# The end of a feed-forward block: turning the next norm's first rows by DMA, and keeping one product's weights for another

## The chip, the cores and the metric

The kernel runs on one core of a Trainium2 chip. The metric is the device time of one execution in microseconds, the median of several runs. TensorE (PE) multiplies, VectorE (DVE) and ScalarE (ACT) work elementwise, GpSimd (POOL) and SyncE (SP) mostly issue transfers here, and the transfers run on 16 DMA engines. Each engine executes its own list of instructions in order.

## The reference

Two layers, each of three residual updates of `x` (512 positions by 1024 channels, float32), and a final norm:

```python
for l in range(DEPTH):                                   # DEPTH = 2
    x = x + 0.5 * swiglu(rms_norm(x, ffn1_norm[l]), ffn1_w_in[l], ffn1_w_out[l])
    x = x + mixer(rms_norm(x, mix_norm[l]), ...)         # attention over a grid, a 2-D DFT, gates
    x = x + 0.5 * swiglu(rms_norm(x, ffn2_norm[l]), ffn2_w_in[l], ffn2_w_out[l])
return rms_norm(x, final_norm)

def swiglu(x, w_in, w_out):                              # w_in 1024 x 5632, w_out 2816 x 1024
    g, u = jnp.split(x @ w_in, 2, axis=-1)
    return (jax.nn.silu(g) * u) @ w_out
```

There are thus four feed-forward blocks (FFNs). The change touches the second product, `(silu(g) * u) @ w_out`, of each.

## The kernel before, in words

**Precision.** Every large product is made of three TensorE passes over float32 values that are split into a high and a low part: high by high, high by low, low by high. A weight granule of 128 x 1024 (or 128 x 512) is loaded into a tile `raw`; ScalarE writes its high part `whi` (line 191, or 186 with the sign turned) and VectorE the low part `wlo` (line 194 or 187). There are three buffers each for `whi` and `wlo`, so granules are prepared two ahead of the one that TensorE works on. Lines 502, 503 and 505 are the three passes.

**Seven products.** The products are done by a Strassen scheme: the two operands are cut into 2 x 2 blocks, and seven products (numbered 1 to 7) of sums and differences of blocks take the place of eight. In the output product of an FFN the 2816 hidden features are cut into two halves of three chunks (3, 4 and 4 tiles of 128). The order is product 1 for its three chunks, then product 2 for its three, then for each chunk the products 5, 6, 7 and 3, and last product 4 for its three: 21 steps, `i` = 0 to 20 in the code. This text calls these 21 steps the end of an FFN. `hl` and `comb` (lines 322, 323 and 744) prepare the activations of a step (`c1h`, `c1l` and so on), `update` (line 750) adds a finished product to `x` from PSUM, on VectorE.

**Weights.** The blocks of `w_out` are called a, b, c and d. Product 1 uses -a, product 2 uses b, product 5 uses d - c, of which c comes by a second transfer that adds to the tile already loaded (GpSimd's queue, line 150; the sign is in the data), product 6 adds a to that, product 7 uses c and a in the same way, product 3 adds b on VectorE (line 164), product 4 uses d alone. Each product loads what it needs anew, so b is loaded for product 2 and once more for product 3. Plain loads are issued by SyncE (line 148) into the tile `raw`, of which there are nine in an FFN. A list of items in the order of use (`stage_items`) says what is loaded when; `Stream.fetch` loads up to eight items ahead of the one being prepared.

**Hidden features to columns.** The last hidden blocks of the up phase have to be turned before the end can use them. `apart` copies a block's 16-bit words apart on ScalarE (line 347, tile `zs`), a transposing DMA issued by SyncE (line 348) turns them into `zt`, and `joined_words` puts the words together again (line 357, two copies). In the end this happens for two blocks, z2 and then z1, joined behind the steps 3 (z1) and 5 (z2).

**The next norm's rows.** The next stage needs `x` turned as well, in four quarters, `quad(i, j)`. Each quarter takes eight TensorE transposes of 128 x 128 into PSUM (line 414), four ScalarE copies with the norm's gain (line 417), and a split into high and low part (418 and 419). In the ends of the first three FFNs `quad(0, 0)` stands behind step 6, `quad(1, 1)` and `quad(0, 1)` behind the first step of product 4. The last FFN has none of these: it goes over to the final norm instead. The turned halves are kept in tiles of the tags `xh` and `xl`, two buffers each (8 KB a partition). The current norm's own halves sit in them until the up phase has ended.

**Order.** Except in blocks that are marked as scheduled by hand, the order of instructions on each engine is made by a planner when the kernel is built: it issues an instruction when its operands and a free buffer are there, in the order of the program among those that are ready. `tc.keep_in_program_order` pins an instruction behind those traced before it on its engine.

## Time and profile before

| | |
|---|---|
| three runs | 1849.15, 1852.43, 1852.99 us; median 1852.43 |
| the profiled execution | 1849.34 us, of which 1847.6 us lie between its first and last instruction (the span) |
| mean granted TensorE clock | 0.998 |
| the ends of the four FFNs, from their first matmul to the end of the last | 107.47, 107.48, 108.71 and 105.15 us |
| they begin in the span at | 219.57, 816.28, 1135.32 and 1734.10 us |
| read from HBM | 367.88 MB |

All numbers of the trace are of one profiled execution, and positions are microseconds from the start of its span. A row of the timeline begins with the start and the duration of one instruction (or of several alike, with their count), then engine, line, operation, and the tiles written and read; in square brackets stands how long the engine was idle before, and what ended that. `PEld` is the loading of the stationary operand, `SPq` and `POOLq` are transfers issued by SyncE and GpSimd. Matmuls are pipelined, so one lasts 0.39 us while the next starts after some 0.23. In the rows by group, the number behind the bar is busy time in us, then the mean of one in ns.

### The profile page before, as it was taken

Reading aid. Unit: us, or ns where it says so; the run is one execution under the profiler, and the core shown is the slowest. Engines: PE = TensorE matmul, PEld = TensorE weight load, DVE = VectorE, ACT = ScalarE, POOL = GpSimd, SP = SyncE. Lnnn points to the kernel's source line nnn. Section 1 sums busy time; section 2 is a strip of 40 time slices with the busy share of each in tenths; the row PEclk is TensorE's granted clock in tenths of the full one; section 3 lists DMA queues with packets and bytes.
Section 4 is the critical chain, followed back from the end, with each engine's and each line's share of the span. In section 5 each row is a group of like instructions: output and inputs, shape, how many; then the busy total and the mean of one; then the engine's idle time right before and its main releaser. Section 6 shows DMA issues by size and latency. Waiting matters only on the chain.

```text
span 1847.6 us, 24580 instructions
## 1 busy us (share of the span) xinstructions
PE 1836.8 (99%) x8850; PEld 1528.9 (83%) x8850; DVE 1603.4 (87%) x1950; ACT 1312.9 (71%) x1785; POOL 173.3 (9%) x212
## 2 busy tenths in 40 slices
PE   9999999999999999999999999999999999999998
PEld 7888888888888888888888888888888888888886
DVE  7878899786989987889998888997869899888899
ACT  6777875668576777777667778766776776777865
POOL 0010010100111010001010100101001101010010
PEclk9999999999999999999999999999999999999999
DMA  9898799934897798979888886989258866989795
GB/s 306 223 236 218 192 276 272 229 107 125 232 235 174 183 220 222 213 203 280 248 194 221 223 223 195 270 285 213 69 183 212 227 176 170 236 219 223 199 285 150
DMA packets 198282, 395.72 MB, mean 214 GB/s; under 512 B 103760, under 2 KB 103888, under 8 KB 198160
## 3 DMA queue, kind: packets, MB, share of 16 engines
q1 hardware_dynamic: 168912, 294.23, 50.2%
q0 software_dynamic: 28816, 99.38, 30.0%
q8 instruction: 69, 1.13, 0.2%
q10 hardware_dynamic: 432, 0.55, 0.1%
q14 instruction: 53, 0.43, 0.1%
HBM read 367.88 MB, written 2.11 MB: 200 GB/s over the span
## 4 chain that ended last, share of the span: by engine, by line
PE 96%; DVE 2%; ACT 1%; issue 0%; DMA 0%; SPq 0%; DVEq 0%; ACTq 0%
PE A L502 10%; PE A L505 10%; PE A L503 10%; PE o L505 7%; PE o L503 7%; PE o L502 7%; PE B L502 5%; PE B L503 5%; PE B L505 5%; PE ps L316 4%; PE ps L317 3%; PE ps L318 3%; PE C L503 3%; PE C L502 3%; PE C L505 3%; PE tr L414 1%
## 5 line engine op out<-in xcount | busy, mean ns | idle before, releaser
L194 DVE TENSOR_TENSOR wlo<-raw,whi 128x1024 fp32r<-128x1024 f32 (+1 forms) x534 | 630.3, 1190 | 176.4 <-ACT whi L191 175.8
L191 ACT ACTIVATE whi<-raw 128x1024 fp32r<-128x1024 f32 (+1 forms) x534 | 546.0, 1033 | 256.5 <-PE A L503 53.8
L150 POOL DMA_DIRECT2D raw<-in_wst_dram x166 | 144.4, 894 | 1350.9 <-DMA raw<-in_wst_dram 810.8
L164 DVE TENSOR_TENSOR raw<-raw,raw 128x1024 f32<-128x1024 f32 (+1 forms) x148 | 176.1, 1190 | 2.0
L503 PE MATMUL A<-whi,xl 128*128 128x512 f32 x400 | 155.7, 389 | 0.0
L502 PE MATMUL A<-whi,xh 128*128 128x512 f32 x400 | 155.7, 389 | 0.0
L357 ACT ACTIVATE at<-zt 128x1024 uint16<-128x1024 uint16 (+2 forms) x96 | 110.4, 1167 | 15.6 <-DMA zt<-zs 15.4
L186 ACT ACTIVATE whi<-raw 128x1024 fp32r<-128x1024 f32 (+1 forms) x83 | 85.8, 1037 | 46.9 <-issue 12.8
L505 PE MATMUL A<-wlo,xh 128*128 128x512 f32 x400 | 115.1, 389 | 0.0
L187 DVE SCALAR_TENSOR_TENSOR wlo<-raw,whi 128x1024 fp32r<-128x1024 f32 (+1 forms) x83 | 98.2, 1191 | 12.1 <-ACT whi L186 12.1
L505 PEld LDWEIGHTS A<-wlo,xh 128*128 128x128 f32 x400 | 75.1, 188 | 15.6
L503 PEld LDWEIGHTS A<-whi,xl 128*128 128x128 f32 x400 | 75.1, 188 | 15.5
L502 PEld LDWEIGHTS A<-whi,xh 128*128 128x128 f32 x400 | 75.1, 188 | 15.4
L503 PE MATMUL C<-whi,xl 128*128 128x512 f32 x208 | 81.0, 389 | 0.0
L503 PE MATMUL B<-whi,xl 128*128 128x512 f32 x208 | 81.0, 389 | 0.0
L502 PE MATMUL C<-whi,xh 128*128 128x512 f32 x208 | 80.9, 389 | 0.0
L502 PE MATMUL B<-whi,xh 128*128 128x512 f32 x208 | 80.9, 389 | 0.0
L347 ACT ACTIVATE zs<-th 128x1024 uint16<-128x1024 uint16 x80 | 79.5, 1041 | 0.8 <-DVE th L731 0.8
L724 ACT ACTIVATE th<-sn,rh 128x512 f32<-128x512 f32 x80 | 55.0, 715 | 34.2 <-DVE sn L577 33.4
L572 ACT ACTIVATE sn<-A 128x512 f32<-128x512 f32 x104 | 59.1, 585 | 25.1 <-PE A L505 25.0
L505 PE MATMUL C<-wlo,xh 128*128 128x512 f32 x208 | 59.8, 389 | 0.0
L505 PE MATMUL B<-wlo,xh 128*128 128x512 f32 x208 | 59.8, 389 | 0.0
(428 smaller groups left out, 4680.5 us busy)
## 6 DMA issues: line engine op xcount, KB each, us to landing
raw<-in_wst_dram SPq DMA_DIRECT2D x468, 512.0 KB, 5.9
raw<-in_wst_dram POOLq DMA_DIRECT2D x176, 512.0 KB, 7.9
bm<-in_bias_dram SPq DMA_DIRECT2D x16, 512.0 KB, 4.3
raw<-in_wst_dram SPq DMA_DIRECT2D x30, 256.0 KB, 4.1
x<-in_xin_dram SPq DMA_DIRECT2D x4, 512.0 KB, 10.2
raw<-in_wst_dram POOLq DMA_DIRECT2D x8, 256.0 KB, 8.8
dft<-in_dft_dram POOLq DMA_DIRECT2D x8, 256.0 KB, 11.1
gb<-in_gbias_dram SPq DMA_DIRECT2D x4, 512.0 KB, 9.1
```

The lines of the kernel that those rows point to most:

```text
L150: G.dma_start(out=self.t, in_=wst[GRAN_AT[self.plus]][:, 0 : self.n], accum_op=ALU.add)
L164: V.tensor_tensor(self.raw.t, self.raw.t, self.add.t, ALU.add)
L186: S.activation(hi, t, AF.Copy, scale=-1.0)
L187: self.last = V.scalar_tensor_tensor(lo, t, -1.0, hi.bitcast(F32), ALU.mult, ALU.subtract)
L191: S.activation(hi[:, cs], t[:, cs], AF.Copy)
L194: self.last = V.tensor_tensor(lo[:, cs], t[:, cs], hi[:, cs].bitcast(F32), ALU.subtract)
L316: PE.matmul(ps, lh, rh, start=start, stop=False, skip_group_check=again)
L347: S.activation(s[:, h], words[:, h], AF.Copy)
L357: S.activation(to[:, w], t[:, w], AF.Copy)
L502: PE.matmul(ps, lh, rh, start=start, stop=False, skip_group_check=again)
L503: PE.matmul(ps, ll, rh, start=False, stop=False, skip_group_check=again)
L505: PE.matmul(ps, lh, rl, start=False, stop=stop, skip_group_check=again)
```

## The change

**Product 2's weights.** The six granules of block b (three chunks, two granules each) are made once per FFN, as `kept`, and both product 2 and product 3 use them. They have a home instead of a `raw` tile: two tiles of the tag `xh` and one of `xl`, that is, buffers in which the current norm's halves lay. They are loaded by GpSimd's queue. `fetch` stops in front of such an item until `homes[0]` is set, which is done at the beginning of the end; behind step 6 it is taken back.

**The next norm's first rows.** `quad(0, 0)` no longer uses TensorE. `turned_quad` does it in five pieces behind the steps 6, 8, 10, 11 and 12: words apart on ScalarE, the transposing DMA on SyncE (in program order), words joined on ScalarE, four scalings by the gain on ScalarE (from SBUF, in place), the split on ScalarE and VectorE. The words before and after the turn lie in the second `xl` buffer. The other two quarters of an end stay as they are, and so does the last FFN in this respect.

```diff
-                self.t = raw_pool[0](self.n)
+                self.t = homes[0](*self.home, self.n) if self.home else raw_pool[0](self.n)
+                queue = G if self.home else nc.sync
...
-                    nc.sync.dma_start(out=self.t[:, cs], in_=wst[GRAN_AT[self.key]][:, cs])
+                    queue.dma_start(out=self.t[:, cs], in_=wst[GRAN_AT[self.key]][:, cs])
...
+            if kept:
+                r["b"] = kept
...
+            kept = [
+                [Raw((s, "ob", c, g), n, home=(c, g)) for g, n in enumerate(out_sizes(c))] for c in range(3)
+            ]
             for order in ((1,), (2,), (5, 6, 7, 3), (4,)):
                 for c in range(3):
                     summed = s == (L - 1, 2) and c == 2
-                    strassen(s, lambda q: "o" + q, c, out_sizes(c), order, summed)
+                    strassen(s, lambda q: "o" + q, c, out_sizes(c), order, summed, kept=kept[c])
...
             while self.loaded < min(to, n) and self.items[self.loaded].stage <= self.stage:
+                if self.items[self.loaded].raw.home and not homes[0]:
+                    break
...
+        def turned_quad(self, i, j, st):
+
+            js = slice(j * 256, (j + 1) * 256)
+            s = st[:, 0].rearrange("p (h q b f) -> p h q b f", h=2, q=4, b=2)
+            t = st[:, 1].rearrange("p (h q c) -> p h q c", h=2, q=4)
+            words_apart(x[:, 2 * j : 2 * j + 2, i * T : (i + 1) * T], s)
+            yield
+            tc.keep_in_program_order(turned_words(s, t)[1])
+            yield
+            raw = self.raw[i, j] = slot(F32, "xr")
+            joined_words(raw, t)
+            yield
+            self.tiles(i)
+            for k in range(4):
+                S.activation(raw[:, k, :], raw[:, k, :], AF.Copy, scale=self.gain(4 * i + k))
+            yield
+            split(self.h[i][:, :, js], self.l[i][:, :, js], raw)
+            yield
...
+        kept = [np_.tile([P, 4, T], F32, tag="xh", name=nm("ob"), bufs=2) for _ in range(2)]
+        words = np_.tile([P, 2, 2048], U16, tag="xl", name=nm("zq"), bufs=2)
+        kept.append(np_.tile([P, 4, T], F32, tag="xl", name=nm("ob"), bufs=2))
+        homes[0] = lambda c, g, n: kept[c][:, 2 * g : 2 * g + n // T, :].rearrange("p k t -> p (k t)")
+        quad00 = nxt.turned_quad(0, 0, words)
...
-            if i == 6 and not late:
-                nxt.quad(0, 0)
+            if i == 6:
+                homes[0] = None
+            if i in (6, 8, 10, 11, 12) and not late:
+                next(quad00)
```

In the last FFN's third chunk product 3 takes b by an adding transfer in both versions; there the change only moves product 2's load. `apart` is split into `words_apart` and `turned_words`, with the same work.

More of the change, by code (lines that the diff above doesn't have):

```diff
@@ L203, in add, with strassen @@
             items.append(Item(*a, stage=st, **k))
-        def strassen(s, name, idx, sizes, order, dma=False, behind=None):
+        def strassen(s, name, idx, sizes, order, dma=False, behind=None, kept=None):
             def key(q, g):
@@ L313, in encoder_kernel @@
     raw_pool = [None]
+    homes = [None]
     def mm3(ps, lh, ll, rh, rl, start, stop, again=False):
```

16 lines of the change are left out of this document (10 added, 6 removed).

## Prediction

> **What bounds the kernel now.** I read the page's first part, then the four stretches in which the change acts, then the timelines inside them. "End 1" to "end 4" are the four output products of the FFNs, from their first matmul to their last; a "step" is one of an end's 21 (product, chunk) pairs, a "granule" one load of 128x1024 or 128x512 weights.
>
> ```profile
> span 1847.6 us, 24580 instructions
> PE 1836.8 (99%) x8850; PEld 1528.9 (83%) x8850; DVE 1603.4 (87%) x1950; ACT 1312.9 (71%) x1785; POOL 173.3 (9%) x212
> core 0: us, PE busy (x) PEld busy (x) DVE busy (x) ACT busy (x) POOL busy (x), PEclk, DMA share, GB/s
> 219.57:327.04 107.47, 107.47 (x488) 89.25 (x486) 104.21 (x108) 77.26 (x97) 12.63 (x15) 1.00 0.95 269
> 816.28:923.76 107.48, 107.48 (x488) 89.25 (x486) 106.90 (x111) 78.00 (x98) 12.96 (x15) 1.00 0.92 256
> 1135.32:1244.03 108.71, 108.33 (x487) 88.94 (x486) 104.29 (x108) 76.84 (x97) 12.56 (x15) 1.00 0.93 264
> 1734.10:1839.25 105.15, 105.15 (x463) 86.38 (x461) 101.70 (x116) 71.27 (x87) 12.12 (x14) 1.00 0.81 219
> ```
>
> Over the whole span TensorE is the bound. In the ends it has company: in end 2 VectorE works 106.90 of 107.48 us, and the DMA engines are over nine tenths busy in three of the four. So a microsecond taken from TensorE there counts only where VectorE is early enough. How early it is stands in the timelines of VectorE and TensorE at the last granule of product 3, where `wlo` is written by line 194 and read by line 505 (ends 1, 2 and 3):
>
> ```profile
> 306.60 1.22 DVE L194 TENSOR_TENSOR wlo<-raw,whi 128x1024 fp32r<-128x1024 f32 x1
> 308.45 0.62 PE L505 MATMUL o<-wlo,c3h 128*128 128x512 f32 x2
> 903.23 1.21 DVE L194 TENSOR_TENSOR wlo<-raw,whi 128x1024 fp32r<-128x1024 f32 x1
> 905.17 0.62 PE L505 MATMUL o<-wlo,c3h 128*128 128x512 f32 x2
> 1223.30 0.98 PE L505 MATMUL o<-wlo,c3h 128*128 128x512 f32 x3 [0.38 <-DVE wlo L194]
> ```
>
> In end 1 the low part is ready at 306.60 + 1.22 = 307.82 and used at 308.45: 0.63 us to spare. In end 2 it is 905.17 - 904.44 = 0.73. In end 3 it comes too late, and TensorE sits idle. That is the first thing to keep in mind: the margins are under a microsecond.
>
> **The change part by part.** *Transposes leave TensorE.* Three ends (not the fourth, which has no next norm to prepare) lose the eight transposes of the next norm's block (0, 0):
>
> ```profile
> 253.57 1.03 PE L414 MATMUL tr<-ident,x 128*128 128x128 f32 x8
> 254.36 0.49 PE L502 MATMUL o<-whi,c6h 128*128 128x512 f32 x1
> 254.68 0.40 PE L503 MATMUL o<-whi,c6l 128*128 128x512 f32 x1
> ```
>
> From 253.57 to the next matmul it is 0.79 us, and that one is followed after 0.32 instead of about 0.23 as elsewhere: 0.88 us an end, 2.6 us in all. The transposes stand ahead of product 3, and VectorE's work up to there is the same in number: the split of the block (one 1.2 us operation) only moves from behind step 6 to behind step 12. So TensorE would reach product 3's last granule 0.88 us earlier and wait there for what VectorE lacks. Realised: 0.63 in end 1, 0.73 in end 2, nothing in end 3. Term one: **-1.4 us**.
>
> *ScalarE takes over the turning.* Each of the three ends gets two copies of 16-bit words, one DMA transpose, two copies that join them; the four scalings stay, now from SBUF.
>
> ```profile
> L347 ACT ACTIVATE zs<-th x80: 1036/1042/1060, 69.8 to 1742.1; 128x1024 uint16<-128x1024 uint16 x80
> L357 ACT ACTIVATE at<-zt x96: 477/1358/1380, 82.9 to 1758.0; 128x1024 uint16<-128x1024 uint16 x64, 128x256 uint16<-128x256 uint16 x16, 128x768 uint16<-128x768 uint16 x16
> L348 SPq DMA_TRANSPOSE zt<-zs x44: 1346/3350/7060, 71.9 to 1743.2; - x44
>   DMA zt<-zs: 15.4, 8
> ```
>
> That is 2 x 1.04 + 2 x 1.36 = 4.8 us of ScalarE an end. The cover is its idle time, 107.47 - 77.26 = 30 us in end 1, so I put it at nothing. If a copy stands just ahead of a `whi` that VectorE waits for, VectorE loses up to the 1.36 us of that copy; the last row (idle time before line 357 by releaser) says that where the wait is for the transposing DMA it was 15.4 / 8 = 1.9 us each, in 8 cases. On SyncE the new transpose stands in program order behind the loads issued by step 8, and holds the queue 3.35 us in the middle; the loads behind it are later by that, but see the next part.
>
> *Six loads fewer an end, six on another queue.* Product 3 no longer loads its second addend; product 2 loads it once, to tiles that the up phase has left, on GpSimd's queue.
>
> ```profile
> raw<-in_wst_dram SPq DMA_DIRECT2D x468, 512.0 KB, 5.9
> raw<-in_wst_dram POOLq DMA_DIRECT2D x176, 512.0 KB, 7.9
> zt<-zs SPq DMA_TRANSPOSE x44, 5.4
> dft<-in_dft_dram POOLq DMA_DIRECT2D x8, 256.0 KB, 11.1
> 1792.06 2.01 ACT L191 ACTIVATE whi<-raw 128x1024 fp32r<-128x1024 f32 x2 [3.19 <-DMA raw<-in_wst_dram]
> 1793.16 1.23 DVE L194 TENSOR_TENSOR wlo<-raw,whi 128x1024 fp32r<-128x1024 f32 x1 [2.52 <-ACT whi L191]
> 1194.60 1.23 DVE L194 TENSOR_TENSOR wlo<-raw,whi 128x1024 fp32r<-128x1024 f32 x1 [0.60 <-ACT whi L191]
> ```
>
> Five loads of 512 KB and one of 256 KB go away, 2.9 MB of the some 29 MB (107.47 us x 269 GB/s) of an end; in the last end only two chunks of three gain. More than that, these granules leave the nine `raw` buffers, for which SyncE's loads queue, so the loads of products 5, 6 and 7 start earlier. Late landings show in the last three rows: VectorE idle 2.52 us in end 4 and 0.60 in end 3. End 3 gets back its 0.60. End 4 has 462 matmuls; the chain of waits shows 24 of them in
>
> ```profile
> 268.72 0.91 PE o L505 x4
> 274.16 0.91 PE o L505 x4
> ```
>
> 5.44 us, so 462 take 104.8, and 105.15 - 104.8 = 0.35 is all that end 4 can return. Term two: **-0.95 us**.
>
> *The dead tiles' price.* The loads of product 2 were in flight before the end began; now the first may start only when the up phase has read its last, about the end's first matmul. ScalarE wants the first granule 11.2 us into end 1 (230.78):
>
> ```profile
> 230.78 1.56 ACT L191 ACTIVATE whi<-raw 128x1024 fp32r<-128x1024 f32 x2
> 234.27 1.07 ACT L191 ACTIVATE whi<-raw 128x1024 fp32r<-128x1024 f32 x1 [0.98 <-PE o L503]
> 235.24 2.58 ACT L357 ACTIVATE at<-zt 128x1024 uint16<-128x1024 uint16 x2
> GB/s 131 323 225 16 66 104 296 313 89 27 120 290 283 120 315 357 270 281 296 80 60 230 285 197 219 203 241 263 274 356 411 422 413 375 219 192 224 219 142 219
> ```
>
> With 7.9 us to landing it is there after some 9 us, so the weights themselves cost nothing. Below, an earlier start could gain at most the 0.8 us that VectorE idles early in end 1; above, by the 11.1 us of the nearest plain load on that queue, it would be about 12 us, near 1 us late. But the last row (40 slices of 0.75 us of 219.57 to 249.50) shows where they run: beside the two transposes of the last hidden block, issued 3.1 and 9.1 us into the end. The second is what line 357 needs at 235.24, and ScalarE is in order: behind it stands `whi` of product 2's second chunk. End 3 already shows what a transfer on GpSimd's queue does beside that transpose:
>
> ```profile
> 1144.39 3.20 SPq L348 DMA_TRANSPOSE zt<-zs  x1
> 1146.83 1.73 POOL L150 DMA_DIRECT2D raw<-in_wst_dram  x2 [49.58 <-DVE at L744]
> 1151.98 2.59 ACT L357 ACTIVATE at<-zt 128x1024 uint16<-128x1024 uint16 x2 [0.89 <-DMA zt<-zs]
> 1155.51 1.23 DVE L194 TENSOR_TENSOR wlo<-raw,whi 128x1024 fp32r<-128x1024 f32 x1 [1.81 <-ACT whi L191]
> 829.72 2.59 ACT L357 ACTIVATE at<-zt 128x1024 uint16<-128x1024 uint16 x2 [1.23 <-DMA zt<-zs]
> 238.75 1.23 DVE L194 TENSOR_TENSOR wlo<-raw,whi 128x1024 fp32r<-128x1024 f32 x1 [0.80 <-ACT whi L191]
> ```
>
> The block arrived about 1151.98, 7.6 us after its issue, and VectorE stood still 1.81 us instead of end 1's 0.80; those 1.0 us are most of the 1.24 by which end 3 is longer than end 1. I bound this cost by nothing (the slices at 3 and 6 to 8 us into the end, with 16 and 27 GB/s, have room for all of it) and by 3 us an end (below). Nearest is end 3's row: 1.0 us each for ends 1 and 4. End 2 waited 1.23 for the block and lost no VectorE time early (busy in all of 816.28 to 846.20), so 0; end 3 has paid. Term three: **+2.0 us**.
>
> The Trainium skill, "DMA: Bandwidth & Descriptors", section "Issuing engines are not separate DMA queues", says that DMAs started by any engine run on the same 16 DMA engines and interleave; "Queues, rings and completion order" adds that each engine goes round-robin between the queue rows by packets. End 3's rows agree (the turned block landed later beside GpSimd's transfer). By that rule alone the second transpose would halve its rate as long as product 2's weights flow, which speaks against this change and is the first rival below.
>
> **Sum.** -1.4 - 0.95 + 2.0 = -0.3 us on the profiled execution's own 1849.34 (span 1847.6): 1849.0. That execution stands 3.1 us under the median of the three runs, 1852.43, so on the median it is 1852.1.
>
> **The rivals.** *Slower: the last hidden block is late in every end.* GpSimd's ring then has up to six loads in flight from about 1 to 12 us. At end 1's 269 GB/s, 2.9 MB take 10.8 us; if a third falls ahead of the second transpose, it lands 3.6 us later. ScalarE waits, VectorE idles as long, and it has no time to give back (104 to 107 of 107 us). Minus what the row of end 1 leaves, about 3 us an end: 4 x 3 = 12, with the first two terms +9.7: about 1862. It decides where the block lands later than 15.7 us into the end. For it: the 0.89 and 1.23 us waits exist today. Against: the empty slices, and two dead tiles (product 3 of the up phase was their last reader) free 5 us before the end.
>
> *Faster: everything asked for is realised.* More prefetch keeps VectorE from ever idling; then 2.6 + 1.24 + 0.35 = 4.2 us go, 1848.2. For it: the margins are missed by tenths only. Against: end 2's VectorE has 0.58 us idle in all, so its share could come only from work that moves behind the end.
>
> *Slower: the turned rows are late for ScalarE.* The new joining copies come two steps (8.2 us) behind their DMA, which lands after 5.4 us in the middle if SyncE's queue is free. If not, 1.9 us each by the idle row, up to twice in three ends: +5 to +11 with VectorE full, 1857 to 1863 before the other terms.
>
> *Slower: GpSimd's weights late for product 2.* TensorE waits if the first granule lands later than about 13.5 us into the end; at 2 us an end, +8: 1860.
>
> Per "DMA: Bandwidth & Descriptors" of the Trainium skill, "Anatomy of one DMA", a 512 KB load would take about 2.0 + 524288 / 436e3 = 3.2 us (an estimate); by it the last rival falls away, but the rows here say 5.9 and 7.9.
>
> **How the numbers follow.** Forecast 0.37, its own range 1849 to 1856. Late hidden block 0.24, late turned rows 0.07, late weights 0.05: slower together 0.36. Faster 0.27, though its price lies only just outside 0.2% (3.7 us), which is about what this kernel's measurement tells from no change; the three runs themselves lie 3.8 us apart, so an end without late landings could give more on the median than in this profile. The range reaches from just under the faster case to most of the late hidden block: 1847.5 to 1861.
>
> **What would show it.** 72 - 24 = 48 transposes in the ends at line 414's place, ScalarE some 14 us busier, DMA some 10 MB less. Right: TensorE idle before `wlo` in product 3 of ends 1 and 2 of some 0.2 us, and ends of about 107. Wrong to the slow side: line 357 idle for the DMA in the first 20 us of every end, or `xr` copies waiting for it. Wrong to the fast side: ends 1 to 3 near 106.5 us, VectorE never idle in them.

## The result and the profile after

The changed kernel takes 1913.63 us in the median (1892.33 to 1921.82, six runs) against 1851.95 us of the kernel before on the same chip: slower by about 62 us, where 1852.1 was forecast. The ratio, which leaves out the slowest of the six runs because it was in a slower state, is 1.0308, with a 95% interval from 1.0282 to 1.0335. The profiled execution took 1911.5 us, its span is 1909.7 us, 62.1 more than before.

The page's first part, then the stretches of the four ends (from first matmul to last) in the same columns as before:

```profile
span 1909.7 us, 24487 instructions
PE 1845.7 (97%) x8826; PEld 1533.8 (80%) x8826; DVE 1603.6 (84%) x1950; ACT 1325.1 (69%) x1797; POOL 186.2 (10%) x236
220.12:334.51 114.39, 109.61 (x480) 90.37 (x479) 103.91 (x108) 79.81 (x97) 11.95 (x15) 0.97 0.88 255
824.61:952.42 127.81, 108.99 (x479) 89.87 (x478) 106.02 (x110) 81.77 (x102) 12.25 (x15) 0.92 0.86 198
1163.98:1287.77 123.79, 108.83 (x479) 89.83 (x478) 103.82 (x108) 79.25 (x97) 11.99 (x15) 0.93 0.86 210
1781.76:1901.33 119.57, 106.59 (x463) 87.29 (x461) 101.74 (x117) 71.77 (x87) 11.40 (x14) 0.94 0.77 179
```

VectorE has the same work as before (1603.6 against 1603.4 us), and three of the four ends move fewer bytes (end 1 moves 29.1 MB, before 28.9). Still the ends are 6.9, 20.3, 15.1 and 14.4 us longer, together 56.8 of the 62.1. A further 3.9 us lie between end 3 and end 4 (from 1287.77 to 1781.76 it is 493.99 us, before it was 490.07). In the ends TensorE is no longer busy all the time, and its granted clock fell. The waits of TensorE and ScalarE say where (engine, what was waited for; us in total, times, the longest):

```profile
PE o L538 <- ACT whi L192: 51.5, 4, 18.8
ACT at L374 <- DMA zt<-zs: 76.7, 10, 21.2
```

There is one wait of TensorE in each end, four in all, and 51.5 us together. ScalarE's wait for the transposing DMA (line 374 is the old line 357) rose from 15.4 us in 8 cases to 76.7 in 10. The timeline of end 2, which begins at 824.61, shows how the one becomes the other. ScalarE, then TensorE, then what SyncE and GpSimd issue:

```profile
836.15 0.63 ACT L192 ACTIVATE whi<-ob 128x512 fp32r<-128x512 f32 x1 [0.26 <-PE o L539]
858.02 2.53 ACT L374 ACTIVATE at<-zt 128x1024 uint16<-128x1024 uint16 x2 [21.24 <-DMA zt<-zs]
861.54 1.04 ACT L192 ACTIVATE whi<-ob 128x1024 fp32r<-128x1024 f32 x1
862.64 0.79 PE L538 MATMUL o<-whi,c2h 128*128 128x512 f32 x1 [18.82 <-ACT whi L192]
827.68 11.24 SPq L362 DMA_TRANSPOSE zt<-zs  x1
839.63 16.28 SPq L362 DMA_TRANSPOSE zt<-zs  x1
819.19 2.15 POOL L149 DMA_DIRECT2D ob<-in_wst_dram  x4 [0.65 <-PE B L539]
821.31 0.93 POOL L151 DMA_DIRECT2D raw<-in_wst_dram  x1
825.08 1.08 POOL L149 DMA_DIRECT2D ob<-in_wst_dram  x2 [2.83 <-PE A L541]
833.16 0.88 POOL L151 DMA_DIRECT2D raw<-in_wst_dram  x1 [7.01 <-DVE wlo L188]
835.02 0.87 POOL L151 DMA_DIRECT2D raw<-in_wst_dram  x1 [0.97 <-DVE wlo L188]
```

The first transpose holds SyncE for 11.24 us, so the second is issued at 839.63, 15 us into the end instead of 9, and it holds SyncE for another 16.28 us. ScalarE, in order, waits 21.24 us for the turned block, and behind that stands the `whi` that TensorE needs. On GpSimd's queue there are not only product 2's six plain loads (`ob`, line 149): the adding loads of the products 5 and 7 (line 151) come at -3.3, +8.5 and +10.4 us of this end, and one more before that, at -6.9. In the kernel before, the first adding load of this end came at +10.9. Between its issue and its landing the trace has for the two transposes 26.6 and 18.4 us (5.2 and 4.3 before). What the DMA engines did from 837 to 850 us (bytes a second in 40 slices, then packets, MB and share of the 16 engines by queue; q1 is SyncE's, q0 GpSimd's):

```profile
GB/s 71 54 24 26 25 24 23 28 23 71 19 31 37 50 293 58 49 37 44 35 35 22 58 54 69 28 162 121 58 55 81 68 55 102 50 83 109 101 147 93
q1 hardware_dynamic: 1210, 0.33, 85.3%
q0 software_dynamic: 167, 0.51, 43.5%
```

The engines are counted as busy throughout, and move 0.84 MB in 13 us. So this is no shortage of bandwidth: transposes and the other transfers hold each other up. In the ends 3 and 4 it is alike (26.1 and 25.3 us for the first transpose). End 1 is another case: the first transpose took 17.0 us there while the engines moved 4.74 MB, at 278 GB/s, so the many bytes beside it are enough to explain its delay.

After each wait TensorE is slow for some microseconds. These are the stretches of the wait, of the 5 us behind it, and of what follows (the last three columns are granted clock, DMA share and GB/s):

```profile
843.00:862.50 19.50, 0.81 (x4) 0.35 (x2) 0.83 (x1) 4.45 (x5) 1.70 (x2) 0.59 1.11 160
862.50:867.50 5.00, 4.86 (x12) 3.85 (x13) 4.73 (x6) 5.00 (x6) 0.00 (x0) 0.53 0.89 170
867.50:890.00 22.50, 22.50 (x101) 18.60 (x100) 22.50 (x26) 16.06 (x23) 0.85 (x1) 1.00 0.48 119
```

With the clock at 0.53, twelve matmuls start in 5.0 us, 427 ns apart instead of 227. Over the four ends 40 matmuls start late in this way, 8.5 us together. 51.5 of waiting and 8.5 of slow clock are 60.0; the ends grew by 56.8, so some 3 us were gained in them elsewhere. The experiments find these 3 us again.

### The profile page after: what moved, and what is told of

It is laid out like the page before. It is cut to its first block, busy times and chain, and to the rows that moved or that the text cites. A ratio compares the mean times of both kernels' runs of the same rounds, so it can differ in the third digit from the quotient of the medians.

```text
span 1909.7 us, 24487 instructions
## 1 busy us (share of the span) xinstructions
PE 1845.7 (97%) x8826; PEld 1533.8 (80%) x8826; DVE 1603.6 (84%) x1950; ACT 1325.1 (69%) x1797; POOL 186.2 (10%) x236
## 4 chain that ended last, share of the span: by engine, by line
PE 93%; DMA 3%; ACT 2%; DVE 1%; issue 0%; SPq 0%; DVEq 0%
PE A L538 10%; PE A L541 10%; PE A L539 10%; PE o L538 7%; PE o L539 7%; PE o L541 7%; PE B L539 5%; PE B L538 5%; PE B L541 5%; PE ps L325 3%; PE ps L326 3%; PE ps L327 3%; DMA zt<-zs 3%; PE C L538 2%; PE C L539 2%; PE C L541 2%
## 5 line engine op out<-in xcount | busy, mean ns | idle before, releaser
L195 DVE TENSOR_TENSOR wlo<-raw,whi 128x1024 fp32r<-128x1024 f32 (+1 forms) x510 | 603.2, 1192 | 169.8 <-ACT whi L192 169.3
L192 ACT ACTIVATE whi<-raw 128x1024 fp32r<-128x1024 f32 (+1 forms) x510 | 522.4, 1035 | 245.9 <-PE A L539 56.3
L374 ACT ACTIVATE at<-zt 128x1024 uint16<-128x1024 uint16 (+2 forms) x96 | 110.1, 1164 | 76.8 <-DMA zt<-zs 76.7
L165 DVE TENSOR_TENSOR raw<-raw,raw 128x1024 f32<-128x1024 f32 x126 | 151.4, 1202 | 2.0
L187 ACT ACTIVATE whi<-raw 128x1024 fp32r<-128x1024 f32 (+1 forms) x83 | 85.7, 1035 | 45.7 <-issue 12.5
L538 PE MATMUL o<-whi,c2h 128*128 128x512 f32 x88 | 38.6, 439 | 51.5 <-ACT whi L192 51.5
L538 PEld LDWEIGHTS A<-whi,xh 128*128 128x128 f32 x400 | 75.1, 188 | 15.4
L538 PEld LDWEIGHTS o<-whi,c2h 128*128 128x128 f32 x88 | 18.8, 213 | 57.3 <-ACT whi L192 53.2
## 6 DMA issues: line engine op xcount, KB each, us to landing
ob<-in_wst_dram POOLq DMA_DIRECT2D x20, 512.0 KB, 11.6
```

The source lines that it names most:

```text
L165: V.tensor_tensor(self.raw.t, self.raw.t, self.add.t, ALU.add)
L187: S.activation(hi, t, AF.Copy, scale=-1.0)
L192: S.activation(hi[:, cs], t[:, cs], AF.Copy)
L195: self.last = V.tensor_tensor(lo[:, cs], t[:, cs], hi[:, cs].bitcast(F32), ALU.subtract)
L374: S.activation(to[:, w], t[:, w], AF.Copy)
L538: PE.matmul(ps, lh, rh, start=start, stop=False, skip_group_check=again)
```

## The experiments

In each of them the kernel before ran on the same chip. "T1" and "T2" are the two transposes of the last hidden block; positions with a sign count from the start of an end. Issue and landing are those of the single transfer in the trace.

### Which half of the change

`turn` leaves the weights as they were, `keep` leaves the next norm's rows as they were:

```diff
# turn: product 2 and 3 load b into raw tiles, no homes
-                    strassen(s, lambda q: "o" + q, c, out_sizes(c), order, summed, kept=kept[c])
+                    strassen(s, lambda q: "o" + q, c, out_sizes(c), order, summed)
# keep: the first quarter is turned on TensorE
-            if i in (6, 8, 10, 11, 12) and not late:
-                next(quad00)
+            if i == 6 and not late:
+                nxt.quad(0, 0)
```

> Only the next norm's first rows are turned by a DMA; product 2's and product 3's weights are loaded by SyncE into raw tiles as before the change. Theory 1 (the last hidden block's transposing DMA is starved by transfers on GpSimd's queue, which only the kept weights bring forward): no end has TensorE idle for more than 1 us before product 2's second chunk, the time is 1847 to 1853 us. Theory 2 (the new transpose and its copies on ScalarE are what makes the ends late): the ends keep at least half of what they lost, above 1880 us.

> Only product 2's weights are kept for product 3, in the dead tiles and on GpSimd's queue; the next norm's first rows are turned on TensorE as before the change. Theory 1 (last hidden block's transposing DMA starved): TensorE idle 4 to 19 us in each end before product 2's second chunk, 1905 to 1925 us, as with the whole change. Theory 2 (the new transpose): about 1852 us.

Measured: `keep` 1907.85 us, 1.0315 [1.0255, 1.0374]; `turn` 1870.99 us, 1.0118 [1.0087, 1.0148]. With `keep`, TensorE waits in the same four places:

```profile
PE o L538 <- ACT whi L192: 38.9, 4, 13.5
```

So the kept weights carry the loss, and theory 2 falls. But `turn` isn't free either, though theory 1 had it so (1847 to 1853 us). There T1 and T2 land as before (T2 at +13.4 to +15.1), and it is the new transpose `zq` that ScalarE waits for; that is taken up again below.

### Which transfers: the queue, or the earlier adding loads

```diff
# sync: the kept weights on SyncE's queue
-                queue = G if self.home else nc.sync
+                queue = nc.sync
# held: a kept granule also occupies a raw tile until its high part is made
+                if self.home:
+                    self.d = raw_pool[0](self.n)
+                    nc.sync.dma_start(out=self.d[:, 0:16], in_=wst[GRAN_AT[self.key]][:, 0:16])
...
+            if self.raw.home and self.raw.d is not None:
+                S.activation(self.raw.d[:, 0:16], self.raw.d[:, 0:16], AF.Copy)
```

> The whole change, but product 2's kept weights are loaded by SyncE's queue into the same dead tiles. Theory 1a (the six plain loads on GpSimd's queue starve the transposes): the last hidden block lands within 18 us of the end's start, TensorE waits under 2 us an end, 1850 to 1860 us. Theory 1b (it is the adding loads of product 5 on GpSimd's queue, which start up to 15 us earlier because six granules no longer take raw tiles): they still start early, the block still lands more than 20 us into the end, above 1885 us.

> The whole change, with GpSimd's queue for product 2's weights, but each of the six granules also holds a raw tile (64 bytes a row of it are loaded by SyncE, and ScalarE copies them in place after the granule's high part), so the loads that follow get their raw tiles no earlier than before the change. Theory 1a (plain loads on GpSimd's queue starve the transposes): stalls of 4 to 19 us an end stay, above 1890 us. Theory 1b (adding loads too early): the adding loads start 11 us or more into an end, the block lands within 18 us, 1850 to 1862 us.

Measured: `sync` 1857.47 us, 1.0029 [1.0013, 1.0045]; `held` 1889.04 us, 1.0227 [1.017, 1.0283]. TensorE's wait at the disputed place, for `sync` and then for `held`:

```profile
PE o L538 <- ACT whi L192: 2.7, 1, 2.7
```

```profile
PE o L544 <- ACT whi L195: 19.4, 4, 8.1
```

`sync` is in the range that 1a gave, and T2 lands at +16.5 to +17.3. But it does not separate the two theories: two adding loads of GpSimd still start ahead of each end there (-7.0 to -4.2), and the next only at +15.1 to +15.9, where the change has them at +6.8 to +8.5. `held` lies between the two theories: its adding loads start at +4.3 to +6.5 instead of -6.9, but still 6 to 8.5 us earlier than before the change, and T1 lands at +16.9 to +19.1. `held` also has a disturbance of its own, 1.3 to 3.2 us an end in product 1, whose loads queue behind the raw tiles. Neither theory alone gives both numbers. What the kernels have in common is when GpSimd's queue runs empty in the first part of an end (the second row is a run of the next part):

| kernel, end | last transfer of GpSimd's batch lands | T1 lands |
|---|---|---|
| `held_best` (below), ends 1 to 4 | +8.0 to +10.1 | +11.8 to +12.1 |
| `dose_g`, end 4 | +12.3 | +14.0 |
| `keep`, end 1 | +18.0 | +19.4 |
| the change, end 1 | +18.7 | +20.1 |
| the change, end 2 | +30.6 | +29.7 |

### The disputed cost by itself

The kernel before gets extra loads of 512 KB at the start of the ends, into the dead tiles, used by nobody: none in end 1, then 2, 4 and 6. `dose_g` issues them from GpSimd, `dose_a` from ScalarE, `dose_s` from SyncE, whose queue also carries the transposes; `dose_p` pairs a plain load by SyncE with an adding one by GpSimd. `dose_g12` and `dose_s12` have 4, 8 and 12 of them. `dose_split` is `dose_s` with T1 and T2 issued by ScalarE.

```diff
         ps = {}
+        spare = [np_.tile([P, 4, T], F32, tag=t, name=nm("sp"), bufs=2) for t in ("xh", "xh", "xl")[3 - extra[0] :]]
+        for t in spare:                      # the 12s: spare + spare
+            for g in range(2):
+                G.dma_start(                 # dose_a: S; dose_s: nc.sync; dose_p: nc.sync, then G with accum_op=ALU.add
+                    out=t[:, 2 * g : 2 * g + 2, :].rearrange("p k t -> p (k t)"),
+                    in_=wst[GRAN_AT[((0, 1), "ob", 2, g)]][:, 0:1024],
+                )
+        extra[0] += 1
# dose_split, also
-            turned.append((apart(z), j, f0))
+            turned.append((apart(z, S if f0 == 2 + 4 * (NB - 1) else None), j, f0))
```

> The kernel before, with 0, 2, 4 and 6 plain loads of 512 KB in the ends 1 to 4, issued by GpSimd at the end's start into the dead tiles and used by nobody. It prices GpSimd's queue beside the two transposes of the last hidden block with nothing else moved. If transfers on GpSimd's queue starve a transpose: the block lands 2 to 4 us after the last of them, later from end to end, and ends 3 and 4 lose 2 to 10 us each. If only bytes count (2.1 MB more in end 3, 3.1 MB in end 4, against some 29 MB): the block lands at most 3 us later and no end loses over 3 us.

> The same 0, 2, 4 and 6 extra loads, issued by ScalarE. If any second queue beside SyncE's starves the transposes, the block lands as late as with GpSimd's loads; if it is GpSimd's queue alone, the block lands within 18 us of the end's start in all ends. ScalarE stands at the loads until the dead tiles are free, so some of the time may be its own wait.

> The same 0, 2, 4 and 6 extra loads, issued by SyncE ahead of the transposes on their own queue. If it is a second queue beside the transposes that starves them, the block lands within 18 us of the end's start in all ends, later only by the time that the loads take (under 3 us), and the ends lose under 2 us each.

> The kernel before, with 0, 2, 4 and 6 pairs of extra loads in the ends 1 to 4: a plain load of 512 KB by SyncE into a dead tile, and an adding load of 512 KB by GpSimd on top of it; nobody uses them. If adding loads are what starves a transpose, end 3 and end 4 lose clearly more than with as many plain loads on GpSimd's queue (which lost nothing in end 3 and some 3.5 us in end 4): the block lands more than 20 us into end 4, and end 4 loses 5 to 20 us. If adding and plain loads on GpSimd's queue are alike, end 3 loses under 2 us and end 4 under 5.

> The kernel before, with 0, 4, 8 and 12 plain loads of 512 KB by GpSimd at the start of the ends 1 to 4, each destination written twice in the ends 2 to 4; nobody uses them. If any transfer on GpSimd's queue holds a transpose back, the first transpose of end 4 lands 1 to 2 us after the last of the twelve, about 20 us into the end, and end 4 loses 5 us or more. If only adding loads do, it lands within 12 us although the plain loads are still under way. If the mutual slowing needs adding loads, the twelve take no more than some 12 us each and end 4 loses under 10 us, against 29.8 us with six adding loads.

> The kernel before, with 0, 4, 8 and 12 plain loads of 512 KB by SyncE, the queue of the transposes, at the start of the ends 1 to 4 (the second half of them overwrite the first). If the queue matters and not the bytes, a transpose takes 4 to 8 us from its issue in every end, and what is lost is that it is issued later, behind the loads. If bytes matter, the first transpose of end 4 takes 15 us or more, as with twelve by GpSimd (20.3 us).

> The kernel before, with the two transposes of the last hidden block issued by ScalarE instead of SyncE, and 0, 2, 4 and 6 plain loads of 512 KB by SyncE at the start of the ends 1 to 4. If any queue beside the transposes' own holds them back, the first transpose of end 4 takes 9 us or more and lands shortly after SyncE's loads have landed, and already in end 1 it takes longer than the 7.7 us of before, since SyncE's usual loads are now on another queue. If it is GpSimd's queue alone, it takes 4 to 8 us in every end. ScalarE stands while it issues a transpose, so some time is lost that way.

Measured, a single time each, with the kernel before at 1849.91 to 1850.54 us beside them. The ends of the profile before were 107.48, 108.71 and 105.15 us (2 to 4), and T1 took 5.1 us in end 4:

| kernel | time, us | ends 2, 3, 4, us | T1 in end 4: issue to landing, us |
|---|---|---|---|
| `dose_g` | 1853.3 | 107.65, 107.97, 108.56 | 11.0 |
| `dose_a` | 1856.8 | 107.47, 109.73, 112.18 | 11.7 |
| `dose_s` | 1854.16 | 110.73, 107.58, 107.21 | 5.2 |
| `dose_p` | 1894.61 | 114.07, 117.31, 134.91 | 29.9 |
| `dose_g12` | 1881.1 | 109.56, 116.40, 126.62 | 20.3 |
| `dose_s12` | 1864.21 | 108.50, 111.77, 114.58 | 4.3 |
| `dose_split` | 1892.41 | 127.38, 113.73, 114.47 | 11.6 |

The rows behind the last column for `dose_s12`, `dose_g12` and `dose_split`, each from the answer for the moment at which T1 of end 4 is issued:

```profile
zt<-zs SPq DMA_TRANSPOSE x1, 4.3
```

```profile
zt<-zs SPq DMA_TRANSPOSE x1, 20.3
```

```profile
zt<-zs ACTq DMA_TRANSPOSE x1, 11.6
```

- Twelve loads on the transposes' own queue leave them as fast as they were (T1 4.3 us, T2 5.5); the same twelve on GpSimd's make T1 take 20.3. This does not show that bytes are not the cause, as its expectation would have it. SyncE issues in order: of the twelve in end 4 of `dose_s12` only two were under way when T1 was issued and two more were issued before it landed, and 1.08 MB moved in that time, about as much as before the change (1.11 MB); in `dose_g12` it was 5.39 MB. Where more loads of its own queue ran beside T1, it was slower too: in end 2 of `sync`, with five of SyncE's loads under way at its issue, it took 8.0 us and 2.46 MB moved (0.05 of them GpSimd's); in end 2 of `wait` (next part), with four of GpSimd's and three of SyncE's, 8.8 us and 2.38 MB. The rows of these two:

```profile
zt<-zs SPq DMA_TRANSPOSE x1, 8.0
zt<-zs SPq DMA_TRANSPOSE x1, 8.8
```

- What `dose_s12` loses in its ends 3 and 4 it loses by late weights, which queue behind the extra loads.
- It need not be adding loads either, as I had thought after `dose_g`, where six plain ones were over at +12.3 and cost 3.4 us in end 4, and four cost nothing in end 3 (neither of its expectations). Twelve plain ones on GpSimd's queue, the last of which land at +29.9, cost end 4 21.5 us, six adding ones 29.8. With the plain ones, too, the engines count as busy and slow down: from +15 to +21 of that end they move 84 GB/s, and T1 lands at +23.3, ahead of the last four. The adding ones need the plain ones below them first, so they begin late: five of the six land between +7.8 and +34.6, the sixth is only issued at +36.2.
- Nor is it GpSimd. In `dose_a` T1 lands at +14.3, 1.4 us after the last of ScalarE's loads, as with GpSimd's (+14.0, 1.7 us after). In `dose_split` the transposes are on ScalarE's queue, and now SyncE's loads hold them back: T1 takes 8.0, 7.9, 11.8 and 11.6 us with 0, 2, 4 and 6 extra loads, and no transfer of GpSimd beside it in the first three. When GpSimd's adding loads come as well, T2 takes up to 25.2 us.

So a transpose is held back by the loads that run beside it, whichever engine issued them. Its own queue helps in so far as SyncE, which issues in order, lets few loads run beside it; whether another queue costs more at the same number of bytes these runs do not separate. The expectations of `dose_a` and `dose_split` for GpSimd's queue alone are refuted, except that T2 in `dose_a` still came by +16.2, because six loads were over by then. Both also lose time because ScalarE stands while it issues (2.4 and 3.4 us of TensorE in end 4 of `dose_split`, 3.7 in that of `dose_a`); end 1 of `dose_split`, with no extra load, took 115.06 us, 7.6 more than before. The 3.3 us of `dose_s` in end 2 lie at other places and stay unexplained.

### Without the adding loads, and with them held

`noplus` leaves the ends' adding loads out, so that the products 5 and 7 use d and c alone. `wait` keeps all of the change, and lets the first four adding loads of an end wait for T2; those behind them on GpSimd's queue, which issues in order, wait with them. (In the trace the first of the four is issued 1.0 to 1.4 us before T2 lands, the others behind it.)

```diff
# noplus
-                r[q] = [Raw(key(q, g), n, q2 and key(q2, g)) for g, n in enumerate(sizes)]
+                r[q] = [Raw(key(q, g), n, q2 and not kept and key(q2, g)) for g, n in enumerate(sizes)]
# wait (last_turn[0] is the name of the latest transposing DMA)
-                    G.dma_start(out=self.t, in_=wst[GRAN_AT[self.plus]][:, 0 : self.n], accum_op=ALU.add)
+                    late = G.dma_start(out=self.t, in_=wst[GRAN_AT[self.plus]][:, 0 : self.n], accum_op=ALU.add)
+                    if self.key[1] in ("oc", "od") and self.key[2] == 0:
+                        info = mybir.DependencyInfo(mybir.DependencyClass.Sync, mybir.DependencyReason.DATA)
+                        tc.add_manual_dep(late.ins, last_turn[0], info, reason="after the last turn")
```

> The whole change without the adding loads of the ends: products 5 and 7 use d and c alone, so 12 granules an end are not completed and 48 transfers of 512 KB (256 KB for the short ones) are left out. Product 2's weights stay on GpSimd's queue. If the plain loads alone starve the transposes: TensorE idle 4 us or more in each end before product 2's second chunk. If it needs the adding loads: the block lands some 18 us into the end and TensorE is idle there under 2 us an end; the turned rows then land 6 us after their issue and cost nothing, and the time is under 1856 us.

> The whole change; each end's first four adding loads on GpSimd's queue (the two for product 5's first chunk, the two for product 7's) wait until the second transpose of the last hidden block has landed. Product 2's six plain loads stay on GpSimd's queue. If the plain loads alone starve the transposes, stalls of 4 us and more stay in each end and the time is above 1885 us. If it is adding loads beside transposes, the block lands some 18 us into the end, as in end 4 of the run with six extra plain loads on GpSimd's queue, and each end loses 2 to 4 us there and at product 5, whose weights now come later: 1858 to 1872 us with the turned rows' own loss.

Measured: `noplus` 1854.09 us; `wait` 1854.75 us, 1.0021 [1.0012, 1.003]. Holding back four loads an end takes away 59 of the 62 us, with product 2's weights still on GpSimd's queue. This is better than the 1858 to 1872 us expected of `wait`. The ends of `wait`:

```profile
220.03:326.56 106.53, 106.53 (x479) 88.44 (x478) 103.94 (x108) 79.41 (x97) 13.76 (x17) 1.00 0.94 265
817.06:927.74 110.68, 107.60 (x480) 87.98 (x478) 106.03 (x110) 81.69 (x102) 14.04 (x17) 1.00 0.88 226
1139.30:1245.83 106.53, 106.53 (x479) 88.44 (x478) 103.94 (x108) 79.41 (x97) 13.77 (x17) 1.00 0.88 245
1738.94:1843.66 104.72, 104.72 (x463) 86.52 (x461) 101.76 (x117) 71.82 (x87) 13.18 (x16) 1.00 0.78 202
```

T1 lands at +11.9 in all four, T2 at +14.9 to +16.3. Three ends are now shorter than before the change, by 0.94, 2.18 and 0.43 us. What remains is end 2 (3.2 us longer than before) and the mixer behind end 3, 3.6 us longer than before in `sync` and 3.0 in `wait`.

### The last two places

In end 2, `wait` still has the joining copies of the first block ahead of the `whi` of product 2's second chunk in ScalarE's list, as in the timeline above (836.15, 858.02, 861.54); in the other ends they stand behind it. The kernel before had the same order in end 2 (line 357 at 829.72, +13.4), but there the block came in time. And at the second mixer's start GpSimd's queue stands at the load of `ch`, a table of the mixer. This is GpSimd after the change, and before it:

```profile
1281.58 0.56 POOL L1101 DMA_DIRECT2D ch<-in_chan_dram  x1 [36.72 <-DMA bm<-in_bias_dram]
1282.12 1.77 POOL L151 DMA_DIRECT2D raw<-in_wst_dram  x2
```

```profile
1223.55 0.56 POOL L1058 DMA_DIRECT2D ch<-in_chan_dram  x1 [17.92 <-DVE wlo L194]
1227.95 0.85 POOL L150 DMA_DIRECT2D raw<-in_wst_dram  x1 [3.84 <-PE o L505]
```

Before, `ch` came 20 us ahead of end 3's last matmul (1244.03), after the change 6 us ahead of it (1287.77), and the mixer's first adding loads wait behind it. `held_best` mends both, and `held_keep` does the same without the turned rows:

```diff
                 turned.reverse()
-                joined()
+                with tc.issue_after(ws.items[ws.pos].high.ins):
+                    joined()
...
-        G.dma_start(out=ch, in_=chan)
...
         def constants():
+            tc.keep_in_program_order(G.dma_start(out=ch, in_=chan))
```

> The run with the four adding loads held, and two repairs of order: the copies that join the first of the two turned blocks stand behind the high part of the second chunk's first granule in ScalarE's list in every end (in end 2 they stood ahead of it), and the load of ch stands behind the mixer's first adding loads in GpSimd's queue instead of ahead of them. If these are the two places where the held version loses, end 2 falls from 110.7 to 106.5 us, the second mixer's start gives back 3.6 us, and the time is 1844 to 1849 us, below before. If end 2 and the mixer lose for another reason (DMA bandwidth), the time stays at 1852 to 1856 us.

> As the run with both repairs, but the next norm's first rows are turned on TensorE as before the change. By the working of the prediction the eight transposes cost 0.88 us in each of three ends where VectorE has room: 2.6 us more than with the turned rows. If the gain is the earlier loads alone, it is within 1 us of it.

Measured: `held_best` 1846.72 us, 0.9973 [0.9964, 0.9981]; `held_keep` 1847.49 us, 0.9979 [0.997, 0.9989]. Both are faster than the kernel before (1851.18 us there). The ends of `held_best`, and the longest wait that TensorE has left, which lies outside the ends:

```profile
219.96:326.49 106.53, 106.53 (x479) 88.41 (x478) 103.94 (x108) 79.59 (x97) 13.20 (x16) 1.00 0.93 266
816.73:923.45 106.72, 106.72 (x480) 88.28 (x478) 104.94 (x109) 80.45 (x101) 14.06 (x17) 1.00 0.89 235
1135.01:1241.54 106.53, 106.53 (x479) 88.41 (x478) 103.94 (x108) 79.38 (x97) 13.19 (x16) 1.00 0.92 257
1731.76:1836.48 104.72, 104.72 (x463) 86.52 (x461) 101.77 (x117) 71.74 (x87) 13.19 (x16) 1.00 0.78 202
PE ps L136 <- DVE ones L132: 1.2, 1, 1.2
```

In the ends TensorE is busy without a gap. They sum to 424.50 us, 4.3 less than before (428.81); those of `held_keep` (107.47 three times, and 104.72) to 427.13, 1.7 less. The turned rows are thus worth 2.6 us in the ends, as expected, but only 0.8 us in the median: the two mixers were 0.5 and 0.9 us longer in the profile of `held_best` (490.24 and 490.22 us between the ends, against 489.73 and 489.31), and why is open.

Without GpSimd's queue for the weights, and without the turned rows:

```diff
# keep_sync: keep, and
-                queue = G if self.home else nc.sync
+                queue = nc.sync
```

> Product 2's weights kept for product 3 in the dead tiles, loaded by SyncE, and the next norm's first rows turned on TensorE as before the change. What is left of the change without a load on GpSimd's queue and without the new transpose. If fewer loads help VectorE in the ends: 1845 to 1849 us. If the second transpose, issued about 1 us later behind those loads, costs as much in end 2 as in the run with both (4 us), and the adding loads of the second mixer still start late (3.6 us): 1852 to 1857 us.

Measured: 1858.96 us, 1.0039 [1.0025, 1.0053], above the range given. The second expectation holds in its places (end 2 is 4.9 us longer than before, the mixer's start is late), and end 4 is longer too, by 2.2 us: T2 lands at +17.0 to +17.5 in the ends 1 to 3 and at +19.1 in end 4, because it is issued behind the loads on the one queue. So on SyncE's queue, too, the loads slow the first transpose down (7.7 to 10.0 us, before 5.1 to 7.7), and they make the second one's issue 1.1 to 3.2 us later. What this costs against GpSimd's queue with its adding loads held back is read from `sync` and `wait`, which both have the turned rows and neither of the two mendings: 1857.47 against 1854.75 us.

### The turned rows alone

```diff
# turn_late: turn, and
-            if i in (6, 8, 10, 11, 12) and not late:
+            if i in (6, 8, 12, 13, 14) and not late:
# turn_again: turn once more, for a second profile
```

> Only the turned rows, as in the run with them alone, but the words are joined, scaled and split behind the steps 12, 13 and 14 instead of 10, 11 and 12. If the whole loss of the turned rows is ScalarE waiting for a transpose that takes some 12 us beside GpSimd's transfers, the wait goes: no TensorE idle over 1 us in an end, ends 1 to 3 of 105 to 107 us, 1845 to 1852 us. If the loss is the copies on ScalarE or the place of the transpose in SyncE's queue, the time stays above 1857 us.

> The turned rows alone once more, for a second profile. The first profiled execution (1857.6 us) was the fastest of four, the others took 1867.6 to 1877.1. If the slow executions are those in which the new transpose collapses together with GpSimd's adding loads, a profile above 1865 us shows it landing 20 us or more after its issue in at least one end; in a profile near 1857 us it lands within 13 us everywhere.

Measured: `turn_late` 1868.31 us, 1.0107 [1.0072, 1.0142]; `turn_again` 1868.15 us. ScalarE's wait for the turned rows in the first profile of `turn` (1857.57 us), and in the second:

```profile
ACT xr L374 <- DMA zq<-zq: 8.7, 3, 4.0
```

```profile
ACT xr L374 <- DMA zq<-zq: 15.7, 3, 8.7
```

In the first the new transpose took 12.8, 12.5 and 13.1 us, in the second 17.5, 12.1 and 17.4 (20 us or more was expected of a slow one), with the adding loads of the middle of an end beside it, and TensorE stood still up to 7.2 us. It is the same collapse in another place: from +49.5 to +55.5 of end 3 in the second profile the engines move 56 GB/s and count as busy. It comes in some executions and not in others, which fits the spread of this kernel from 1857 to 1877 us. Joining later did not help: in the profile of `turn_late` (1856.72 us, the fastest of six) nobody waits for `zq` any more, but the transpose holds SyncE's queue (7.10 us in end 1), and the plain loads behind it come late instead:

```profile
286.14 1.06 ACT L192 ACTIVATE whi<-raw 128x1024 fp32r<-128x1024 f32 x1 [3.01 <-DMA raw<-in_wst_dram]
```

With the weights kept (`wait`, `held_best`) six loads fewer stand behind that transpose, it takes 7 to 11 us, and no wait is left.

## Why the prediction was wrong

**The step that failed is "the dead tiles' price", +2.0 us.** It should have been some +60. I looked for what would run beside the two transposes and counted product 2's weights alone. By themselves these are nearly harmless, as forecast: with the adding loads out of the way T1 lands at +11.9, T2 by +16.3, and outside end 2 nothing is lost (`wait`, which takes back 59 of the 62 us). What I did not follow was my own sentence in the part before: that the granules leave the raw tiles, "so the loads of products 5, 6 and 7 start earlier". Half of product 5's and 7's loads are adding ones on GpSimd's queue. They now came up to 18 us earlier, two among the six plain loads and two just behind them, and kept that queue occupied for as long as the first transpose was under way. An earlier load was counted as a gain (term two) and never as traffic.

**The upper bound of 3 us an end failed with it.** It shared bandwidth between the bytes: a third of 2.9 MB ahead of the transpose. In end 1, where the engines kept their rate (278 GB/s), 4.74 MB moved while the first transpose was under way, and TensorE waited 4.8 us. In the ends 2 to 4 it was no sharing any more, and TensorE waited 13.0 to 18.8 us. The Trainium skill, "DMA: Bandwidth & Descriptors", section "Issuing engines are not separate DMA queues", by which transfers of all engines interleave, let me expect that the transpose halves its rate. The traces here disagree with that expectation: the first transpose's time rose from 5.2 to 26.6 us in end 2, and the other transfers slowed down as well (20.2 us each for two adding loads).

**The evidence was in the profile of before.** The page gives one median for all 44 transposes, 5.4 us, and I used that. Single ones differ by a factor of two. These four answers, each for one moment at which a single transpose was issued, are from 663.8, 670.7, 1581.7 and 1588.8 us, the first and third beside two adding loads of GpSimd, the second without, the fourth (two transposes under way) one of each kind:

```profile
zt<-zs SPq DMA_TRANSPOSE x1, 8.8
zt<-zs SPq DMA_TRANSPOSE x1, 4.3
zt<-zs SPq DMA_TRANSPOSE x1, 9.1
zt<-zs SPq DMA_TRANSPOSE x2, 6.7
```

In the first case the later of GpSimd's transfers landed 7.2 us after the issue of the transpose and the transpose 1.6 us later, in the third 7.3 and 1.8. A cost that ends when another transfer ends has no bound of 3 us; it has the bound of that transfer.

**The first rival had the mechanism** (the last hidden block late in every end), with a chance of 0.24, and its limit was about right: the block matters from some 15.7 us on, and in `wait` T2 at 14.9 to 16.1 us cost nothing (in end 2, with its other order, the block matters from some 13.4 us on). Its price was 12 us; it cost 56.8 in the ends. The sign given for the slow side came as well: line 357, now 374, waits for the DMA 7.4 to 21.2 us in every end.

**The other terms held, as far as they could be seen.** Transposes off TensorE: 0.88 us an end was forecast, 0.94, 0.75 and 0.94 were measured (`held_keep` against `held_best`). I had cut this to 1.4 us in all by VectorE's margins; with the loads of the middle earlier those margins were no limit. Fewer loads: 0.60 and 0.35 us for the ends 3 and 4, measured 1.24 and 0.43 (before against `held_keep`). The 0.35 was a slip in the sum: 462 matmuls at 5.44 us for 24 are 104.7 us, which leaves 0.43. The added copies on ScalarE are free, as said, if their transpose is not late; in the change itself nobody waits for it, and the rival of the late turned rows came in `turn` only. The rival "everything asked for is realised" gave 4.2 us; the ends of `held_best` give 4.3.

**Two costs I did not see at all**: that the planner's order in ScalarE's list differs in end 2, as it already did before (with `wait`, 3.2 us), and that the load of `ch` comes later when the raw tiles are taken in another sequence (3.0 to 3.9 us). Mending both took 8.0 us off (1854.75 to 1846.72). The cause of `ch`'s lateness is argued from its wait only; that its memory lay under a raw tile which is now freed later was not tried.

## What to carry to other kernels

Before moving a load, list every transfer whose start depends on the buffer that it frees, with the queue of each, and lay that list over the transposes of the same stretch. A transposing DMA here lands, in most of these cases, some two to three microseconds after the last load that was issued ahead of it, and where loads keep coming while it is under way, all of them can slow down. Keep such loads apart from it by a dependency (`wait`), not by hoping for gaps; its own queue is the weaker remedy (`sync`). And look at single instances of a DMA, with and without each neighbour, before using its median: where the two differ by a factor of two, the neighbour is the price.

## What the runs showed of the hardware that was not expected

- A transpose of 512 KB takes 4.3 to 8.0 us alone or beside up to six plain loads of its own queue. On other queues, two adding loads beside it make that 8.8 to 9.1 us, the six plain ones of `dose_g`, `dose_a` and `dose_split` 11.0 to 11.7, the twelve of `dose_g12` 20.3, the six pairs of `dose_p` 29.9. In the worst stretch all 16 DMA engines count as busy and move some 65 GB/s (0.84 MB in 13 us), where a whole end before moved 256. What happens inside the engines no trace shows.
- The slowing is mutual and lasts: in end 2 two adding loads issued at 833.16 and 835.02 took 20.2 us each. The collapse does not come in every execution (`turn`, 12.8 or 17.5 us for the same transpose).
- After TensorE had waited 3.4 us or more (`held` 3.4, the change 4.8 to 18.8), 6 to 14 of the next matmuls started 427 ns apart instead of 227; behind the waits of the change the granted clock was 0.53 to 0.76 for 5 to 7 us. After a wait of 2.3 us (`turn`, end 1) there are no such rows, after one of 2.6 us with a further pause just behind it (`turn`, end 3) there are eight. The Trainium skill, "TensorE: Matmul & The Clock Gate", section "What's actually happening", gives 3.4 us as the window after which an idle TensorE loses half its clock. The longer waits agree with it; the one of 2.6 us is shorter. In the four ends the slow clock added 8.5 us to the 51.5 us of waiting.
